# Gate and up of 19 of 22 feature tiles by seven block products of a Strassen form

## The chip, the core and the metric

The kernel runs on one core of one Trainium2 chip. The metric is the device time of one execution in microseconds (us), as the median of several runs; the kernel before has 719.12 us (719.12, 715.12 and 721.13). Engines are called as the profile does: PE is TensorE (matmuls), PEld its loading of the stationary operand, DVE VectorE, ACT ScalarE, POOL GpSimd, SP SyncE, whose queue issues the transfers from and to HBM.

## What is computed

One decoder layer over 512 tokens and a width of 1024, in float32: a token mixer (four heads of differential attention and eight of a sparse attention), an output projection, a residual, and a channel mixer. The change concerns the channel mixer alone, which is

```python
x = x + rms_norm(mix, attn_post_norm[l])
h = rms_norm(x, ffn_pre_norm[l])
f = (jax.nn.silu(h @ w_gate[l]) * (h @ w_up[l])) @ w_down[l]
x = x + rms_norm(f, ffn_post_norm[l])
```

with h of 512 x 1024, w_gate and w_up of 1024 x 2816 and w_down of 2816 x 1024.

## The kernel before

**Precision.** Every operand of a large matmul is split in a high part, rounded to the format fp32r, and a low part, the rest; a product is three matmuls: high by high, high by low and low by high. ACT makes the high part of a weight tile (`split_w`, L103 in `to_r`) and DVE the low part (L111).

**Tiles.** The 2816 features are 22 tiles of 128. For a tile, `ff_gate` (L841 to 860) makes gate and up, each with 8 row blocks of 128 of the width and three products: 2 x 8 x 3 = 48 matmuls (L850) of 512 columns, the tokens, with a weight block of 128 x 128 as the stationary operand. Both results lie in a PSUM bank each. Then Exp on ACT (L854), add, reciprocal and a product on DVE (L855 to 857) make silu, L858 multiplies by up, and L859 (ACT) and L860 (DVE) split the result in `ffh` and `ffl`, which are kept for all 22 tiles. Tiles 0 and 1 are made in two halves of 256 tokens, with weights that were loaded and split early (`ws` and `whi`, `wlo` in the rows).

**Ahead of it** stand four token tiles of 128: `norm_post` adds the mixer's parts, normalizes and adds the residual (L797 to 801), `norm_pre` normalizes again (L808 to 814), transposes by PE into two banks `trh` (L819) and splits the transposed tile into `hth` (ACT, L822) and `htl` (DVE, L823), the moving operands of L850. POOL multiplies by the gains (L798, L808). `row_rsqrt` makes the sum of squares (ACT L776, DVE L779) and its root.

**Behind it** `down` (L889) takes the 22 tiles one after the other: 4 token tiles x 2 halves of the width x 3 products, 24 matmuls of 512 columns a tile, in eight banks `acc`. The last three tiles are done row by row, and each finished row of token tiles is normalized and written out.

**Order.** A scheduler orders each engine's instructions by a priority, which is the order of the program save where a block is given a higher one (L801 ff. with `tc.high_priority`); every engine then works through its own list in order, and an instruction that waits holds up those behind it on its engine. Buffers are taken from pools by tag in turn (`raw`, `hi` and `lo` have three each for weights; in PSUM `o` has four banks, `gu` and `tr` two each), and the next user of a buffer waits until the last reader is done. All loads are issued from SP's queue in one order, `wraw` for weights (L96 to 98), 512 KB each.

## Time and profile before

| | |
|---|---|
| median of three runs | 719.12 us (715.12 to 721.13) |
| span of the profiled execution | 717.7 us |
| PE busy | 687.1 us, 96% |
| DVE busy | 487.9 us, 68% |
| ACT busy | 302.3 us, 42% |
| POOL busy | 79.5 us, 11% |
| gate and up of tiles 2 to 21 | 366.35 to 590.35 us |
| down | from 590.35 us |

The profiled execution's own time is its span, 717.7 us, from the first to the last instruction; the runs' times are taken without the profile. "Busy" is the union of the durations of an engine's instructions. A matmul's duration overlaps the next one's, so what one costs is read from the distance of the starts. The granted clock is that part of TensorE's full speed, 2.4 GHz, which the chip allowed in a stretch; 0.50 is 1.2 GHz. In a timeline row, x8 stands for eight instructions that followed one another, the time ahead of the engine is from the first one's start to the last one's end, and square brackets hold the idle time before with what ended it.

### The profile page before, as it was taken

The page shows a single profiled execution, that of the slowest core. Times are in us where ns is not written, and L with a number is a line of the kernel's source. Part 1 is how long each engine was busy: PE and PEld are TensorE (multiplying, and loading weights), DVE is VectorE, ACT ScalarE, POOL GpSimd, SP SyncE. Part 2 cuts the span into 40 slices and gives each one's busy share as a digit, 9 for nine tenths or more (in the row PEclk, how much of TensorE's full clock was granted, in tenths as well). Part 3 has the DMA queues.
Part 4 walks back from the last instruction along what each step waited for, and adds up shares of the span by engine and source line. Part 5 has one row for each costly group of instructions (what it writes and reads, how often), then busy time and mean ns, then how long its engine had stood idle before and what let it go on. Part 6 is the DMA issues. An engine that isn't in the chain of part 4 may idle for free.

```text
span 717.7 us, 9480 instructions
## 1 busy us (share of the span) xinstructions
PE 687.1 (96%) x3553; PEld 568.2 (79%) x3553; DVE 487.9 (68%) x801; ACT 302.3 (42%) x632; POOL 79.5 (11%) x86
## 2 busy tenths in 40 slices
PE   9997999999899988986999999999999999999995
PEld 5976888899688877875988888888888888888884
DVE  4867878886999995769876867768677682222227
ACT  7334444466698965536432232322323322121113
POOL 0000000110854443125100000000000000000000
...
GB/s 315 123 132 287 152 273 309 159 258 45 28 134 60 84 35 5 143 263 1 30 89 88 89 91 106 98 88 89 92 109 94 88 89 89 115 90 88 105 13 117
DMA packets 25981, 83.63 MB, mean 117 GB/s; under 512 B 3408, under 2 KB 4304, under 8 KB 25040
## 3 DMA queue, kind: packets, MB, share of 16 engines
...
## 4 chain that ended last, share of the span: by engine, by line
PE 79%; DVE 12%; ACT 4%; DMA 3%; issue 2%; SPq 0%; DVEq 0%; ACTq 0%
PE gu L850 35%; PE acc L889 15%; PE fm L282 9%; PE dv L356 3%; PE tr L501 2%; PE mixp L676 2%; PE avn L629 2%; PE vg L378 2%; DVE nm L489 2%; PE sc L485 2%; PE sc L486 1%; DMA wraw<-in_wf 1%; PE mix L688 1%; PE av L552 1%; ACT p L491 1%
## 5 line engine op out<-in xcount | busy, mean ns | idle before, releaser
L111 DVE TENSOR_TENSOR wlo<-wraw,whi 128x1024 fp32r<-128x1024 f32 (+2 forms) x96 | 116.4, 1215 | 148.2 <-ACT whi L103 100.8
L103 ACT ACTIVATE whi<-wraw 128x1024 fp32r<-128x1024 f32 (+2 forms) x96 | 100.7, 1052 | 210.5 <-PE gu L850 88.2
L850 PE MATMUL gu<-htl,whi 128*128 128x512 f32 (+1 forms) x352 | 86.3, 385 | 0.0
L850 PE MATMUL gu<-hth,whi 128*128 128x512 f32 (+1 forms) x352 | 86.0, 387 | 0.0
L850 PE MATMUL gu<-hth,wlo 128*128 128x512 f32 (+1 forms) x352 | 85.5, 384 | 0.0
L850 PEld LDWEIGHTS gu<-hth,whi 128*128 128x128 f32 x352 | 64.5, 190 | 14.9 <-ACT hth L822 0.3
L850 PEld LDWEIGHTS gu<-htl,whi 128*128 128x128 f32 x352 | 64.3, 187 | 14.7
L850 PEld LDWEIGHTS gu<-hth,wlo 128*128 128x128 f32 x352 | 64.0, 187 | 14.7
L856 DVE RECIPROCAL silu<-silu 128x512 f32<-128x512 f32 (+1 forms) x24 | 74.0, 3085 | 0.7
L510 POOL TENSOR_TENSOR p<-p,l 128x384 f32<-128x384 f32 (+3 forms) x60 | 49.8, 859 | 144.7 <-DVE l L540 88.3
L491 ACT ACTIVATE p<-sc,nm 128x128 f32<-128x128 f32 (+1 forms) x96 | 50.1, 529 | 20.1 <-DVE nm L489 19.7
L889 PE MATMUL acc<-whi,ffl 128*128 128x512 f32 x144 | 56.0, 389 | 0.0
L889 PE MATMUL acc<-wlo,ffh 128*128 128x512 f32 x144 | 56.0, 389 | 0.0
L889 PE MATMUL acc<-whi,ffh 128*128 128x512 f32 x144 | 55.9, 389 | 0.0
L489 DVE TENSOR_REDUCE nm<-sc 128x1 f32<-128x128 f32 (+1 forms) x96 | 42.5, 482 | 10.4 <-PE sc L487 7.1
L282 PE MATMUL fm<-xh,whi 128*128 128x512 f32 x128 | 34.7, 411 | 5.7 <-ACT whi L103 5.2
L505 ACT ACTIVATE pth<-tr 128x384 fp32r<-128x384 f32 (+1 forms) x60 | 31.5, 526 | 16.8 <-PE tr L501 16.6
L506 DVE TENSOR_TENSOR ptl<-tr,pth 128x384 fp32r<-128x384 f32 (+1 forms) x60 | 34.9, 592 | 3.3 <-ACT pth L505 2.9
L485 PE MATMUL sc<-kst,qst 128*128 128x128 f32 (+2 forms) x96 | 35.3, 368 | 1.5 <-DVE pc L586 1.2
L501 PE MATMUL tr<-ident,p 128*128 128x128 f32 x200 | 33.0, 276 | 1.7 <-DVE ptl L506 0.9
L282 PEld LDWEIGHTS fm<-xh,whi 128*128 128x128 f32 x128 | 24.6, 196 | 12.0 <-ACT whi L103 5.8
L282 PE MATMUL fm<-xh,wlo 128*128 128x512 f32 x128 | 33.4, 393 | 0.0
...
## 6 DMA issues: line engine op xcount, KB each, us to landing
wraw<-in_wg SPq DMA_DIRECT2D x22, 512.0 KB, 3.3
wraw<-in_wu SPq DMA_DIRECT2D x22, 512.0 KB, 3.3
wraw<-in_wd SPq DMA_DIRECT2D x22, 512.0 KB, 3.3
wraw<-in_wf SPq DMA_DIRECT2D x16, 512.0 KB, 5.0
...
wraw<-in_wo SPq DMA_DIRECT2D x8, 512.0 KB, 4.1
```

What stands on the lines that cost most here:

```text
L103: act.activation(dst, src, AF.Copy)
L111: (lo_eng or dve).tensor_tensor(lo[:, :w], raw[:, :w], f32(hi[:, :w]), OP.subtract)
L282: pe.matmul(pt, w[:, k * P:(k + 1) * P], xx[k], start=(n == 0), stop=(n == 3 * NK - 1))
L485: pe.matmul(sv, lhs, kk[:, 0, :w], start=True, stop=False)
L489: dve.tensor_reduce(nm, sv, AX.X, OP.max, negate=True)
L491: act.activation(pt, sv, AF.Exp, bias=nm, accum_out=l[:, i:i + 1])
L501: pe.transpose(tr[:, n * P:(n + 1) * P], pts[i][:, j * P:(j + 1) * P], ident)
L506: dve.tensor_tensor(ptl[:, sl], trv, f32(pth[:, sl]), OP.subtract)
L510: pool.tensor_tensor(p, p, l.to_broadcast(list(p.shape)), OP.mult)
L850: pe.matmul(pt, w_col(ww, k), hx[:, k, s0:s1], start=(n == 0), stop=(n == 3 * NK - 1))
L856: dve.reciprocal(sl, sl)
L889: pe.matmul(acc[i][c], a[f][:, i * P:(i + 1) * P], w[wi][:, c * SEQ:(c + 1) * SEQ], start=(first and n == 0), stop=(last and n == 2))
```

## The change

**Seven products.** For tiles 3 to 21 the width is cut in two halves (c = 0, 1) and the tokens in two halves of 256. The blocks of h are A11, A12 (first tokens; first and second half of the width), A21 and A22; b11 and b21 are gate's weights for the two halves of the width, b12 and b22 up's. Winograd's form of Strassen's product gives the four results from seven products of half the width and half the tokens with

- t1 = b12 - b11, t2 = b22 - t1, t3 = b22 - b12, t4 = b21 - t2 for every tile's weights (`ff_prep`, DVE),
- s1 = A21 + A22, s2 = s1 - A11, s3 = A11 - A21, s4 = A12 - s2 once (`h_sums_a`, `h_sums`, DVE and ACT).

Each product is `block_mul` (L905 to 915): 4 row blocks x 3 parts = 12 matmuls of 256 columns (L912), so 84 for a tile where there were 48 of 512 columns. In the text products 1 to 7 are those of `ff_seven` in its order: b11, t1, b21, t2, t4, b22, t3. They accumulate into the halves of two banks x and y; between them ACT copies three partial results out of x and one out of y (L959, L962, L965, L969), and DVE adds banks and copies (L967, L970). The products' order is fixed by a chain of ordering edges, which are not waits.

**Silu** is now the activation of that name, in `ff_gate` (L897) and, for the product tiles, one tile late (`tail`, L976, behind the next tile's L970). Its table is loaded on ACT before the first one and left after the last one (L980).

**Weights.** ACT and DVE now split t2|t1, t3|b22 and b11|b21 (1024 columns each) and t4 (512): four high parts (L933) and four low parts (L934) for a tile. gate's weights still go through `wraw`; up's go to buffers `wu` that share the tag `ru` with the gains; `t21` shares its two with the `u` of the norms. x2 is written to HBM (`x2d`) and read back for the last sum, so that its four buffers serve as weights in between (tag `big`, eight). The gated results stay unsplit (`ffr`) and are split in the down stage (`down_operands`). Tiles 0 to 2 are made as before.

```diff
+NB = {"big": 8, "ru": 2, "t21": 2}
...
-    def work(name):
-        return A.tile([P, D_MODEL], F32, tag="work", name=name, bufs=4)
     g_post, g_pre = gain(0), gain(1)
-    x2 = [A.tile([P, D_MODEL], F32, name=f"x2_{i}") for i in range(NT)]
+    x2 = [big(f"x2_{i}") for i in range(NT)]
...
+    def h_sums_a(i):
+        a21, a22 = trs[i + 2]
+        hr = [f32(sslot("hr")) for _ in range(2)]
+        for c in range(2):
+            h_, l_ = (f32(t[:, 4 * c:4 * c + 4, i * P:(i + 1) * P]) for t in (hth, htl))
+            dve.tensor_tensor(hr[c].rearrange("p (k t) -> p k t", t=P), h_, l_, OP.add)
+        s1, s3 = (f32(sslot("s")) for _ in range(2))
+        dve.tensor_tensor(s3, hr[0], a21, OP.subtract)
+        act.activation(s1, a21, AF.Copy)
+        dve.tensor_tensor(s1, s1, a22, OP.add)
+        raw4[i] = hr, s1, s3
+    def h_sums(i):
+        hr, s1, s3 = raw4[i]
+        s2, s4 = (f32(sslot("s")) for _ in range(2))
+        dve.tensor_tensor(s2, s1, hr[0], OP.subtract)
+        dve.tensor_tensor(s4, hr[1], s2, OP.subtract)
+        raw4[i] = s3
+        h_split(i, (0, s1), (1, s2), (3, s4))
+    def h_split(i, *js):
+        for j, s in js:
+            h_, l_ = (t[:, :, i * P:(i + 1) * P] for t in sums[j][1])
+            sv = s.rearrange("p (k t) -> p k t", t=P)
+            act.activation(h_, sv, AF.Copy)
+            dve.tensor_tensor(l_, sv, f32(h_), OP.subtract)
+    ffr = [None] * NF
...
-        sl = A.tile([P, SEQ], F32, tag="silu", name="silu", bufs=2)[:, s0:s1]
-        act.activation(sl, pts[0][:, s0:s1], AF.Exp, scale=-1.0)
-        dve.tensor_scalar_add(sl, sl, 1.0)
-        dve.reciprocal(sl, sl)
-        dve.tensor_tensor(sl, sl, pts[0][:, s0:s1], OP.mult)
+        sl = ffr[f][:, s0:s1]
+        with tc.issue_after(getattr(last_exp[0], "ins", last_exp[0])):
+            act.activation(sl, pts[0][:, s0:s1], AF.Silu)
         dve.tensor_tensor(sl, sl, pts[1][:, s0:s1], OP.mult)
-        act.activation(ffh[f][:, s0:s1], sl, AF.Copy)
-        dve.tensor_tensor(ffl[f][:, s0:s1], sl, f32(ffh[f][:, s0:s1]), OP.subtract)
+    def ht_block(t0, c):
+        return [[t[:, 4 * c + k, t0:t0 + HT] for k in range(4)] for t in (hth, htl)]
+    before = [None]
+    def block_mul(pt, w, h, start=False):
+        with ExitStack() as es:
+            if before[0] is not None:
+                es.enter_context(tc.issue_after(before[0]))
+            n = 0
+            for ww, hx in ((w[0], h[0]), (w[0], h[1]), (w[1], h[0])):
+                for k in range(4):
+                    m = pe.matmul(pt, ww[:, k * P:(k + 1) * P], hx[k], start=(start and n == 0),
+                                  stop=(n == 11), skip_group_check=True)
+                    n += 1
+        before[0] = getattr(m, "ins", m)
+    prep = {}
+    def ff_prep(f):
+        rg, ru, t21 = load_w(wg[f]), big("wu", tag="ru"), big("t21", tag="t21")
+        nc.sync.dma_start(ru, wu[f])
+        (b11, b21), (b12, b22) = halves(rg), halves(ru)
+        (t2, t1), t3, t4 = halves(t21), b12, f32(sslot("t4"))
+        ops = prep[f] = {}
+        def operand(names, hl):
+            for j, n in enumerate(names):
+                ops[n] = [t[:, j * SEQ:(j + 1) * SEQ] for t in hl]
+        def split(src, hi, lo):
+            act.activation(hi, src, AF.Copy)
+            dve.tensor_tensor(lo, src, f32(hi), OP.subtract)
+            return hi, lo
+        dve.tensor_tensor(t1, b12, b11, OP.subtract)
+        dve.tensor_tensor(t2, b22, t1, OP.subtract)
+        def home(odd):
+            if f % 2 == odd:
+                return split_slots()
+            return big("wh", F32R), big("wl", F32R)
+        operand(("b11", "b21"), split(rg, *home(1)))
+        dve.tensor_tensor(t3, b22, b12, OP.subtract)
+        dve.tensor_tensor(t4, b21, t2, OP.subtract)
+        operand(("t2", "t1"), split(t21, *home(1)))
+        operand(("t3", "b22"), split(ru, *home(0)))
+        operand(("t4",), split(t4, sslot("t4h"), sslot("t4l")))
+    def ff_seven(f):
+        ops = prep.pop(f)
+        x, y = wide(("o", "gu", "o", "tr")[f % 4], "gw")
+        cy, cx = (f32(sslot(n)) for n in ("cy", "cx"))
+        s1, s2, s3, s4 = (q[0] for q in sums)
+        lo, hi = slice(0, HT), slice(HT, SEQ)
+        block_mul(x[:, lo], ops["b11"], ht_block(0, 0), True)
+        act.activation(cy[:, hi], x[:, lo], AF.Copy)
+        block_mul(y[:, lo], ops["t1"], s1, True)
+        block_mul(y[:, hi], ops["b21"], ht_block(0, 1))
+        act.activation(cx[:, lo], y[:, lo], AF.Copy)
+        block_mul(x[:, lo], ops["t2"], s2)
+        block_mul(x[:, hi], ops["t4"], ht_block(HT, 1))
+        act.activation(cy[:, lo], x[:, lo], AF.Copy)
+        block_mul(y[:, lo], ops["b22"], s4)
+        dve.tensor_tensor(cy, y, cy, OP.add)
+        block_mul(x[:, lo], ops["t3"], s3)
+        act.activation(cx[:, hi], x[:, lo], AF.Copy)
+        dve.tensor_tensor(cx, x, cx, OP.add)
+        if late:
+            late.pop()()
+        def tail():
+            for sl, c in ((lo, cy), (hi, cx)):
+                last = act.activation(c[:, hi], c[:, hi], AF.Silu)
+                dve.tensor_tensor(ffr[f][:, sl], c[:, lo], c[:, hi], OP.mult)
+            if f == NF - 1:
+                with tc.issue_after(getattr(last, "ins", last)):
+                    act.preload_act_table_set("natural_log_exp_and_others")
+        late.append(tail)
...
+    x2d = dram.tile([NT, P, D_MODEL], F32, name="x2d")
+    for i in range(NT):
+        nc.sync.dma_start(x2d[i], x2[i])
...
     ff_gate(0, w0, 0, 256, "gu")
     ff_gate(1, w1, 0, 256, "o")
-    ff_gate(0, w0, 256, SEQ, "gu")
-    ff_gate(1, w1, 256, SEQ, "o")
-    for f in range(2, NF):
-        ff_alloc(f)
-        ff_gate(f, ff_weights(f), 0, SEQ, ("gu", "o", "tr", "o")[f % 4])
+    with tc.issue_after(getattr(scaled[0], "ins", scaled[0])):
+        for i in range(2):
+            h_sums_a(i)
+    ff_gate(0, w0, 256, SEQ, "o")
+    ff_gate(1, w1, 256, SEQ, "gu")
+    for i in range(2):
+        h_sums(i)
+    ffr[2] = f32(sslot("ff2"))
+    w2 = ff_weights(2)
+    ff_prep(3)
+    ff_gate(2, w2, 0, SEQ, "o")
+    for i in range(2):
+        h_split(i, (2, raw4[i]))
+    for f in range(3, NF):
+        ffr[f] = f32(sslot(f"ff{f}"))
+        if f < NF - 1:
+            ff_prep(f + 1)
+        ff_seven(f)
+    late.pop()()
...
+    def down_operands(f):
+        w = split_w(load_w(wd[f]))
+        hi, lo = sslot("ffh"), sslot("ffl")
+        to_r("a", hi, ffr[f])
+        dve.tensor_tensor(lo, ffr[f], f32(hi), OP.subtract)
+        return w, hi, lo
...
+    for i in range(NT):
+        x2[i] = big("x2")
+        nc.sync.dma_start(x2[i], x2d[i])
```

**What stands where, PE.** In the steady state PE had, for one tile, these rows; `hth`, `htl` are h's parts, whi and wlo gate's (bank gu_4497), then up's (gu_4498):

```order
L850 MATMUL gu_4497<-hth_3691,whi_4487 128x512 x8
L850 MATMUL gu_4497<-htl_3692,whi_4487 128x512 x8
L850 MATMUL gu_4497<-hth_3691,wlo_4488 128x512 x8
L850 MATMUL gu_4498<-hth_3691,whi_4493 128x512 x8
L850 MATMUL gu_4498<-htl_3692,whi_4493 128x512 x8
L850 MATMUL gu_4498<-hth_3691,wlo_4494 128x512 x8
```

Now the second half of a tile's row reads as follows: product 4 (t2 by s2, rope_3969), product 5 (t4 by A22), product 6 (b22 by s4, hs_3970) and product 7 (t3 by s3); gw_4713 is bank x, gw_4714 bank y:

```order
L912 MATMUL gw_4713<-rope_3969,wh_4576 128x256 x8
L912 MATMUL gw_4713<-rope_3969,wl_4577 128x256 x4
L912 MATMUL gw_4713<-hth_3695,t4h_4584 128x256 x4
L912 MATMUL gw_4713<-htl_3696,t4h_4584 128x256 x4
L912 MATMUL gw_4713<-hth_3695,t4l_4585 128x256 x4
L912 MATMUL gw_4714<-hs_3970,whi_4580 128x256 x4
L912 MATMUL gw_4714<-hs_3971,whi_4580 128x256 x4
L912 MATMUL gw_4714<-hs_3970,wlo_4581 128x256 x4
L912 MATMUL gw_4713<-hth_3695,whi_4580 128x256 x4
L912 MATMUL gw_4713<-htl_3696,whi_4580 128x256 x4
L912 MATMUL gw_4713<-hth_3695,wlo_4581 128x256 x4
```

Products 4, 5 and 7 go into bank x and 6 into bank y, and product 7 (into the half of x that 4 wrote) is the tile's last.

**ACT.** Before, a tile's list on ACT was Exp, one high part, the split of the tile before, one high part:

```order
L854 ACTIVATE silu_4619<-gu_4569 128x512
L103 ACTIVATE whi_4703<-wraw_4701 128x1024
L859 ACTIVATE ffh7_4555<-silu_4619 128x512
L103 ACTIVATE whi_4709<-wraw_4707 128x1024
L854 ACTIVATE silu_4691<-gu_4641 128x512
```

Now a tile's list has eleven rows; here from the end of one tile (banks gw_4713) to that of the next (gw_4838, gw_4839); `cy` and `cx` are the copies, rows L933 make high parts for the tile two further on, and L976 are the Silus of the tile before:

```order
L933 ACTIVATE whi_4830<-wu_4814 128x1024
L969 ACTIVATE cx_4716<-gw_4713 128x256
L959 ACTIVATE cy_4840<-gw_4838 128x256
L976 ACTIVATE cy_4715<-cy_4715 128x256
L976 ACTIVATE cx_4716<-cx_4716 128x256
L933 ACTIVATE whi_4945<-wraw_4937 128x1024
L962 ACTIVATE cx_4841<-gw_4839 128x256
L933 ACTIVATE whi_4951<-t21_4940 128x1024
L933 ACTIVATE t4h_4959<-t4_4942 128x512
L965 ACTIVATE cy_4840<-gw_4838 128x256
L933 ACTIVATE wh_4955<-wu_4939 128x1024
```

The copy of L965, which reads the half of x that product 4 wrote, stands behind three high parts and cx's copy of L962; it is emitted behind product 5, which writes the same bank, and waits for its end.

**DVE ahead of the tiles.** Before, the last token tile's residual (x2_3) was followed by the reciprocal of tile 0 and then by that token tile's sum of squares (ss_3929):

```order
L801 SCALAR_TENSOR_TENSOR x2_3_3686<-u_3876,rs_3885,x2_3_3686 128x512 x2
L855 TENSOR_SCALAR silu_4013<-silu_4013 128x256
L856 RECIPROCAL silu_4013<-silu_4013 128x256
L779 TENSOR_TENSOR ss_3929<-ss_3929 128x1
L823 TENSOR_TENSOR htl_3692<-trh_3915,hth_3691 128x4x128
L857 TENSOR_TENSOR silu_4013<-silu_4013,gu_3963 128x256
L122 TENSOR_SCALAR rr_3934<-ss_3929 128x1
L823 TENSOR_TENSOR htl_3692<-trh_3916,hth_3691 128x4x128
```

Now three operand sums for tile 3 (L937, L938, L945) stand between them, and behind the scaling of that token tile (mixt_3879) come the sums for s1 to s4, before the low part of its first transposes (trh_3949):

```order
L810 SCALAR_TENSOR_TENSOR x2_3_3690<-u_3880,rs_3889,x2_3_3690 128x512 x2
L937 TENSOR_TENSOR t21_4236<-wu_4235,wraw_4233 128x512
L938 TENSOR_TENSOR t21_4236<-wu_4235,t21_4236 128x512
L945 TENSOR_TENSOR wu_4235<-wu_4235 128x512
L786 TENSOR_TENSOR ss_3933<-ss_3933 128x1
...
L825 SCALAR_TENSOR_TENSOR mixt_3879<-x2_3_3690,rs_3937,gain_3685 128x512 x2
L898 TENSOR_TENSOR ff0_3972<-ff0_3972,gu_3975 128x256
L856 TENSOR_TENSOR hr_4078<-hth_3695,htl_3696 128x512
L856 TENSOR_TENSOR hr_4079<-hth_3695,htl_3696 128x512
L858 TENSOR_TENSOR s_4083<-hr_4078,trh_3919 128x512
L834 TENSOR_TENSOR htl_3696<-trh_3949,hth_3695 128x4x128
```

The sum of squares moved behind work that needs `wu_4235`, a load into the buffer of the first gain, and s_4083 (L858, s3 of the first token tile) reads the bank trh_3919, from the pair of banks that trh_3949 takes next.

## Rows read from the trace of the kernel before

**Rows 1.** The page: its first lines, with busy time, share of the span and instructions of each engine, and the granted clock in 40 slices.

```profile
PE 687.1 (96%) x3553; PEld 568.2 (79%) x3553; DVE 487.9 (68%) x801; ACT 302.3 (42%) x632; POOL 79.5 (11%) x86
```

**Rows 2.** The chain of waits from 300 us on, two of its rows: start, duration, engine, tile, line.

```profile
355.04 235.47 PE gu L850 x1056
590.51 110.20 PE acc L889 x486
```

**Rows 3.** The windows by stage (second halves of tiles 0 and 1; tile 2; tiles 3 to 21; down): length, busy time of each engine (instructions), granted clock, DMA share and GB/s.

```profile
core 0: us, PE busy (x) PEld busy (x) DVE busy (x) ACT busy (x) POOL busy (x), PEclk, DMA share, GB/s
355.04:366.35 11.31, 11.31 (x97) 11.31 (x97) 8.17 (x12) 3.84 (x6) 0.00 (x0) 1.00 0.19 53
366.35:377.55 11.20, 11.20 (x51) 9.00 (x49) 8.82 (x11) 3.56 (x5) 0.00 (x0) 1.00 0.28 90
377.55:590.35 212.80, 212.80 (x914) 170.91 (x912) 152.87 (x134) 63.64 (x76) 0.00 (x0) 1.00 0.29 94
590.35:700.71 110.36, 110.36 (x488) 91.39 (x487) 26.06 (x23) 20.79 (x20) 0.00 (x0) 1.00 0.25 81
```

**Rows 4.** The timeline of PE from 338 us: matmuls of 256 columns (tiles 0 and 1, second tokens) and of 512 columns (tile 2).

```profile
356.08 1.09 PE L850 MATMUL gu<-hth,ws 128*128 128x256 f32 x8
357.02 1.09 PE L850 MATMUL gu<-hth,whi 128*128 128x256 f32 x8
357.95 1.09 PE L850 MATMUL gu<-hth,ws 128*128 128x256 f32 x8
...
366.35 2.03 PE L850 MATMUL gu<-hth,whi 128*128 128x512 f32 x8
368.22 2.03 PE L850 MATMUL gu<-htl,whi 128*128 128x512 f32 x8
370.08 2.03 PE L850 MATMUL gu<-hth,wlo 128*128 128x512 f32 x8
```

**Rows 5.** The groups of instructions by line and form from 355.04 to 590.35 us, those of DVE and ACT that recur in the change: count, busy time, mean ns of one, and the idle time before them.

```profile
L856 DVE RECIPROCAL silu<-silu 128x512 f32<-128x512 f32 x20 | 67.0, 3352 | 0.7
L111 DVE TENSOR_TENSOR wlo<-wraw,whi 128x1024 fp32r<-128x1024 f32 x41 | 50.2, 1224 | 50.0 <-PE gu L850 47.4 <-ACT whi L103 2.6
L103 ACT ACTIVATE whi<-wraw 128x1024 fp32r<-128x1024 f32 x42 | 44.5, 1059 | 88.2 <-PE gu L850 88.2
L858 DVE TENSOR_TENSOR silu<-silu,gu 128x512 f32<-128x512 f32 x19 | 12.9, 680 | 0.0
L860 DVE TENSOR_TENSOR ffl<-silu,ffh 128x512 fp32r<-128x512 f32 x16 | 11.1, 693 | 11.2 <-ACT ffh L859 11.2
L859 ACT ACTIVATE ffh<-silu 128x512 fp32r<-128x512 f32 x16 | 10.1, 633 | 43.1 <-DVE silu L858 43.1
L859 ACT ACTIVATE ffh<-silu 128x256 fp32r<-128x256 f32 x3 | 1.3, 418 | 6.3 <-DVE silu L858 6.3
L857 DVE TENSOR_TENSOR silu<-silu,gu 128x256 f32<-128x256 f32 x3 | 1.2, 410 | 0.0
L854 ACT ACTIVATE silu<-gu 128x256 f32<-128x256 f32 x2 | 0.8, 384 | 1.6 <-PE gu L850 1.6
```

**Rows 6.** The timeline of DVE from 400 us, operations back to back.

```profile
399.59 0.69 DVE L857 TENSOR_TENSOR silu<-silu,gu 128x512 f32<-128x512 f32 x1
400.20 1.22 DVE L111 TENSOR_TENSOR wlo<-wraw,whi 128x1024 fp32r<-128x1024 f32 x1
401.35 0.68 DVE L858 TENSOR_TENSOR silu<-silu,gu 128x512 f32<-128x512 f32 x1
```

**Rows 7.** Transfers: the page's list of DMA issues, and that of 300 to 360 us; the last number is the median us from issue to landing.

```profile
wraw<-in_wu SPq DMA_DIRECT2D x22, 512.0 KB, 3.3
...
gain<-in_grow SPq DMA_DIRECT2D x3, 512.0 KB, 7.2
```

**Rows 8.** The timelines of PE, DVE and POOL from 338 to 358 us, ahead of the steady state.

```profile
339.10 3.79 PE L850 MATMUL gu<-hth,ws 128*128 128x256 f32 x16 [2.98 <-ACT hth L822]
...
353.73 1.29 PE L819 MATMUL trh<-ident,mixt 128*128 128x128 f32 x8
355.04 1.20 PE L850 MATMUL gu<-hth,whi 128*128 128x256 f32 x8
...
347.84 1.75 DVE L856 RECIPROCAL silu<-silu 128x256 f32<-128x256 f32 x1
349.51 0.10 DVE L779 TENSOR_TENSOR ss<-ss 128x1 f32<-128x1 f32 x1
...
352.83 1.41 DVE L814 SCALAR_TENSOR_TENSOR mixt<-x,rs,gain 128x512 f32<-128x512 f32 x2
...
338.64 2.98 POOL L798 TENSOR_TENSOR u<-mixt,gain 128x512 f32<-128x512 f32 x2
341.57 1.28 POOL L808 TENSOR_TENSOR u<-x,gain 128x512 f32<-128x512 f32 x1
```

**Rows 9.** The groups of ACT over the span: the load of an activation table (count, busy us, mean ns).

```profile
L166 ACT ACT_TABLE_LOAD x1 | 1.3, 1283 | 0.7 <-PEq L990 0.7
```

**Rows 10.** The windows of line 850 alone, behind the idle time of rows 8: length, busy time of PE and PEld, granted clock, DMA share and GB/s.

```profile
339.10:342.69 3.59, 3.59 (x17) 3.59 (x17) 0.50 0.02 8
```

**Rows 11.** The timeline of PE from 20 to 32 us: matmuls of 256 columns of another line, first and last of six rows and the next.

```profile
25.92 0.64 PE L356 MATMUL dv<-whi,xh 128*128 128x256 f32 x4
...
28.31 0.64 PE L356 MATMUL dv<-whi,xl 128*128 128x256 f32 x4
28.79 0.64 PE L356 MATMUL dv<-wlo,xh 128*128 128x256 f32 x4
```

More of the change, by code (lines that the diff above doesn't have):

```diff
@@ L105, in to_r, with split_slots @@
             dve.tensor_copy(dst, src)
+    def split_slots():
+        return [wpool.tile([P, 1024], F32R, tag=t, name="w" + t, bufs=b) for t, b in (("hi", WB[1]), ("lo", WB[2]))]
     def split_w(raw, w=1024, lo_eng=None, hi_eng="a"):
-        hi = wpool.tile([P, 1024], F32R, tag="hi", name="whi", bufs=WB[1])
-        lo = wpool.tile([P, 1024], F32R, tag="lo", name="wlo", bufs=WB[2])
+        hi, lo = split_slots()
         to_r(hi_eng, hi[:, :w], raw[:, :w])
@@ L131, in hybrid_block_kernel @@
     S = ctx.enter_context(tc.tile_pool(name="s", bufs=NS, side="left"))
+    pad = ctx.enter_context(tc.tile_pool(name="pad", bufs=1, side="left"))
+    pad.tile([P, 8], F32, name="pad")
     R = ctx.enter_context(tc.tile_pool(name="r", bufs=2, side="left"))
@@ L750, in hybrid_block_kernel, with big @@
     A = ctx.enter_context(tc.tile_pool(name="a", bufs=1, side="right", reuse_waits="tile"))
+    def big(name, dt=F32, tag="big"):
+        return A.tile([P, D_MODEL], dt, tag=tag, name=name, bufs=NB[tag])
     def gain(j):
-        t = A.tile([P, D_MODEL], F32, tag="gain", name="gain", bufs=2)
+        t = big("gain", tag="ru")
         nc.sync.dma_start(t, grow[j].partition_broadcast(P))
@@ L791, in hybrid_block_kernel @@
     mixt, us = [None] * NT, [None] * NT
+    hraw = [None] * NT
     def norm_post(i, mix):
-        mixt[i], us[i] = work("mixt"), work("u")
+        mixt[i], us[i] = big("mixt"), big("u", tag="t21")
         m, u, x_ = halves(mixt[i]), halves(us[i]), halves(x2[i])
@@ L823, in norm_pre, with sum_alloc @@
             dve.tensor_tensor(d_l, tv, f32(d_h), OP.subtract)
-    ffh, ffl, ffw = [None] * NF, [None] * NF, []
-    def ff_alloc(f):
-        for j, (l, n) in enumerate(((ffh, "ffh"), (ffl, "ffl"))):
-            k = 2 * f + j
-            if k < NS:
-                l[f] = sslot(f"{n}{f}")
-            else:
-                k -= NS
-                if k % 4 == 0:
-                    ffw.append(rope_tile())
-                l[f] = ffw[-1][:, k % 4]
+        trs[i] = tr
+    sums, raw4, trs = [], [None, None], [None] * NT
+    def sum_alloc():
+        for j in range(4):
+            if j < 2:
+                t = rope_tile().rearrange("p (s k) t -> p s (k t)", s=2)
+                full = [t[:, s].rearrange("p (k t) -> p k t", t=HT) for s in range(2)]
+            elif j == 2:
+                full = [t[:, :4, HT:] for t in (hth, htl)]
+            else:
+                full = [big("hs", F32R).rearrange("p (k t) -> p k t", t=HT) for _ in range(2)]
+            sums.append(([[t[:, k] for k in range(4)] for t in full], full))
+    def h_sums_a(i):
[23 more added lines that the diff above has]
+    ffr = [None] * NF
     def w_col(w, k):
@@ L862, in hybrid_block_kernel @@
+    late = []
     w0, w1 = st["F0"], st["F1"]
```

29 lines of the change are left out of this document (17 added, 12 removed).

## The prediction

> **What bounds the kernel now.** The page's first rows [rows 1] show TensorE (PE) busy for 687.1 of 717.7 us; the chain of waits says where that decides the end. From 355.04 to 700.7 us its two rows are all PE: 235.47 us of gate and up (L850) and 110.20 us of down (L889) [rows 2]. The windows by stage confirm it: from 355.04 on PE is busy in every microsecond at a granted clock of 1.00, while DVE is busy for 152.87 of 212.80 us and ACT for 63.64 [rows 3]. So a matmul taken out of that stage is time taken out of the kernel, as long as DVE and ACT, which get more to do, stay ahead.
>
> What a matmul costs I read from starts, since durations overlap. Of 512 columns, eight start every 1.866 us (366.35, 368.22, 370.08), 0.2333 us each; of 256 columns, with the same stationary tiles and half the tokens, eight start every 0.933 us (356.08, 357.02, 357.95), 0.1167 us each [rows 4]. Half the columns cost half the time.
>
> **The product tiles.** A tile had 48 matmuls of 512 columns: 48 x 0.2333 = 11.20 us, which is also its step from 366.35 to 377.55 in the windows [rows 3]. It now has 7 products of 12 matmuls of 256 columns: 84 x 0.1167 = 9.80 us, 1.40 us a product. Gain 1.40 us on each of 19 tiles: **-26.6 us**. Tiles 0 to 2 keep their matmuls, and the down stage keeps its 528.
>
> The Trainium skill speaks against this: TensorE: Matmul & The Clock Gate, Back-to-back issue gap, gives a sustained 81 ns at 128 columns and 131 ns at 512, so that narrow matmuls cost more per column. An estimate from these two figures by a straight line, 98 ns at 256 columns, would make the tile 8.2 us against 6.3, a loss of 1.9 us a tile. The trace differs: 0.2333 us at 512 and 0.1167 at 256.
>
> **Does DVE hold the pace?** Per product tile it has: t1 to t4, t4's low part and the two sums over a bank (L967, L970), 7 operations of 512 columns at 0.68 to 0.69 us; three low parts of 1024 at 1.224; two products of 256 at 0.41 [rows 5]: 5 x 0.69 + 2 x 0.68 + 3 x 1.224 + 2 x 0.41 = 9.3 us. Gone are Exp's follow-up with the reciprocal (3.35 us), and two of three 512-column products and splits. Back to back they start closer than they last: the 0.69 us one at 399.59 is followed at 400.20, the 1.22 us one there at 401.35 [rows 6], so 0.61 and 1.15: 7 x 0.61 + 3 x 1.15 + 2 x 0.35 = 8.4 us. Both are under 9.80. The one loop through DVE and ACT: ACT's high part of the gate weights (L933) releases on DVE three low parts, three sums, t4's low part and both bank sums, in that order, 7.1 us; then the second Silu, 0.4; then the next tile's high part, 1.06: 8.6 us, 1.2 under the tile.
>
> **Does ACT hold the pace?** Per tile 3 x 1.059 + 0.633 + 4 x 0.384 + 2 x 0.418 = 6.2 us of 9.80 [rows 5]. Silu is not in the trace; bounds for 256 columns are the nearest rows, 0.384 (Exp from a bank) and 0.418 (Copy from SBUF), and I take the second, which has its operand's place. What matters is ACT's order. Product 7 (t3) accumulates into the half bank that cy's copy (L965) reads, so PE waits for that copy. On ACT there stand ahead of it the gate weights' high part, which waits for the end of product 3 (it overwrites the buffer read there), cx's copy, t21's high part and t4h. From the end of product 3: 1.059 + 0.384 + 1.059 + 0.633 + 0.384 = 3.52 us, against products 4 to 6, 3 x 1.40 = 4.20, less 0.16 by which the last matmul of a run outlasts its slot (1.09 against 0.933 [rows 4]): **0.5 us to spare**. The copy's own wait, for product 5, ends 2 x 1.40 + 0.16 later, and 0.384 behind that is 3.34, less than 3.52. So I price the copies at nothing; their cover is those three products, and what it costs without cover is the third rival. Product 4 overwrites what L959 copied two products earlier, and the bank sums have until the bank comes round, four tiles later.
>
> Transfers: a tile loads two times 512 KB as before, 3.3 us to landing [rows 7]. wu now has two buffers; its load is issued when the low part of the tile two before is read, about 2.3 us into a tile, and is wanted at about 6.5: it lands at 5.6.
>
> **The front.** Here the change costs time. Before, PE was at full supply from 355.04, when the last token tile's transposes (353.73) were through [rows 8]. Now DVE works on t21, t1, t3 of tile 3 ahead of the sum of squares of token tile 3. Their wu uses gain g_post's buffer, free after POOL's last multiply by it; POOL's last operations lie at 338.64 to 342.85 [rows 8], so the load comes at 342.9 + 3.3 = 346.2 and three operations end at 348.3, against 349.51 for that sum before: hidden behind the reciprocal that is gone. mixt of token tile 3 ends at about 352.2 (before 354.24). But its first four transposes now want the bank that s1's copy and s3 (L858) of token tile 0 still read: one product of 256 and three of 512 columns later, 0.4 + 3 x 0.65 = 2.3 us, 354.6, plus ACT's copy, about 354.9 to 355.6 against 353.73. PE resumes 1.2 us later (**+1.2**); the second four transposes come apart, 0.47 us and an idle 0.7 (**+1.2**); the added table load, 1.28 us on ACT [rows 9], stands in that chain, of which I take 0.5 (**+0.5**). Sum **+2.9**. I put the front at 0 at the least (PE has 16 matmuls of the next tiles to put in while it would wait) and at 6.8 at the most (a wu that lands after 7.2 us, as gain's does [rows 7], is 3.9 later, with DVE behind it). PE's granted clock may fall where it idles: after 2.98 idle us it was 0.50 for 3.59 us [rows 8, 10], 1.8 us lost; I expect no idle as long.
>
> **To the down stage.** Its operands' split has moved there. The first, ffh of tile 0, stands on ACT behind the last tile's first Silu, which waits for DVE's sum over the bank of product 6; before, PE went on without a gap at 590.35 [rows 3]. 0.16 + 0.68 + 0.418 + 0.633 = 1.89 us after product 6, of which product 7 covers 1.40: 0.5, with the steps from engine to engine **+0.6** (0 to 2). Per down tile ACT then has 1.059 + 0.633 and DVE 1.224 + 0.693 of 24 x 0.227 = 5.4 us: covered. x2's four reloads stand on SP ahead of the fourth down load and wait there for buffers of product tiles 20 and 21; the first three down tiles, 16 us, cover that, and the rows are wanted 90 us later. The tail is the same.
>
> **Sum.** -26.6 + 2.9 + 0.6 = -23.1 us: 717.7 becomes 694.6 for a profiled execution. The span stood 1.4 under the median of its three runs (715.12 to 721.13), so **696.0** as a median.
>
> **Rivals.**
> A. Narrow matmuls cost more than half. The 256-column ones of L356 start 24 in 2.87 us, from 25.92 to 28.79 [rows 11], 0.1196 each: 84 x 0.1196 = 10.05 us, gain 1.15, so 19 x 0.25 = 4.7 us dearer: 700.8. Against it: these rows run on other operands; the gate's own show 0.1167. (The tile gains nothing from 48 x 0.2333 / 84 = 0.1333 us each.)
> B. DVE becomes the bound. 9.3 us with no overlap and 0.1 us at each of its 12 operations, such as waits for ACT leave, is 10.5 us a tile: 0.7 x 19 = 13.3 more: 709.3. For it: 95% of 9.80 by the means; against it the overlap in rows 6.
> C. The other side: PE waits for the copies out of its own banks. If each of the four in a tile were exposed, matmul's end 0.16 and copy 0.384, that is 0.544 x 4 = 2.18 us a tile, 41 us: 737. It decides from 23.1 / 19 = 1.2 us a tile; product 7 (L968) at L965 is its place, where ACT's chain would have to be 1.7 us longer than 3.52.
> D. The front takes its most, 6.8 us, by a wu load that lands after 7.2 us as gain's did [rows 7]: 696.0 + 3.9 = 699.9.
>
> The Trainium skill, PSUM — Partial Sum Buffer, PSUM bank collisions raise a hardware error, wants readers and writers of a bank kept apart by bank and not by address. By that rule copies of one half would hold up matmuls into the other half of the bank, which is rival C's condition; no row of the kernel before shows such a pair.
>
> **Chances.** Forecast 0.58 (own range 692 to 699: front and down step 0 to 6.5 together), A 0.13, B 0.12, C 0.10 (half of it under 1.2 us a tile), D 0.07. From 690 (no cost in front, a run 2 us under) to 711 (B) holds all but C and a part of B, over 0.8. What this measurement can tell from no change is about 1%, 7.2 us: faster, under 711.9, is forecast, A, D and most of B, 0.86; the rest of B and C's small half within, 0.08; slower 0.06.
>
> **What would show it.** Right: 84 matmuls in 9.8 us from tile to tile at clock 1.00, PE idle nowhere between tile 3 and the last, tile 3 starting at 379.8 to 380.5 (before, 377.55), the last down matmul about 23 us earlier. A: starts 0.1196 apart and no idle. B: idle before L912 ended by L934 or L946 on DVE, DVE above 95% in the stage. C: idle before L912 ended by L965, L959 or L962 on ACT. The forecast is wrong if the tile step is over 10.2 us, or PE's idle in front of tile 3 over 8.

## The result, and the profile after

The changed kernel takes 696.66 us (median of 4 runs, 696.04 to 698.13) against 718.49 us of the kernel before (4 runs beside it): ratio 0.9705, 95% interval 0.9665 to 0.9744. Faster, as forecast, and 0.7 us from the forecast of 696.0. The profiled execution has a span of 695.3 us, 22.4 less than before. The sum came out as forecast, but not all of its terms did: the product tiles gain less than forecast, and the front costs less.

The page's first rows, to be set beside [rows 1]: PE is 25 us less busy, DVE and ACT more.

```profile
PE 662.0 (95%) x4237; PEld 585.9 (84%) x4237; DVE 507.7 (73%) x918; ACT 365.3 (53%) x775; POOL 79.0 (11%) x86
```

The windows by stage (columns as in [rows 3]): the product tiles but for their last 0.7 us, and down but for its last 2.4 us. PE is never idle among the product tiles, at a granted clock of 1.00; DVE has 153.05 of 187.70 us, ACT 104.33.

```profile
378.20:565.90 187.70, 187.70 (x1591) 187.69 (x1590) 153.05 (x213) 104.33 (x183) 0.00 (x0) 1.00 0.35 113
...
567.18:684.40 117.22, 117.22 (x517) 97.06 (x518) 43.79 (x62) 38.16 (x60) 0.00 (x0) 1.00 0.23 74
```

The timeline of PE among the product tiles, from tile 4 and tile 5. Four matmuls with the weights wh or wl start every 0.48 us (386.63, 387.11, 387.59), four with whi or wlo every 0.467 (three times from 396.63 to 398.03): 0.12 and 0.1167 us each.

```profile
386.63 0.64 PE L912 MATMUL gw<-hth,wh 128*128 128x256 f32 x4
387.11 0.64 PE L912 MATMUL gw<-htl,wh 128*128 128x256 f32 x4
387.59 0.64 PE L912 MATMUL gw<-hth,wl 128*128 128x256 f32 x4
...
396.63 0.63 PE L912 MATMUL gw<-hth,whi 128*128 128x256 f32 x4
397.10 0.63 PE L912 MATMUL gw<-htl,whi 128*128 128x256 f32 x4
397.57 0.63 PE L912 MATMUL gw<-hth,wlo 128*128 128x256 f32 x4
398.03 0.63 PE L912 MATMUL gw<-hth,whi 128*128 128x256 f32 x4
```

The timelines of PE and ACT ahead of tile 3, which answer to [rows 8]: the last token tile's transposes wait 0.99 us for ACT's copy of s1, and PE then waits twice 0.69 us for ACT's split; tile 3 starts at 378.20 (before: 377.55). The table load at 347.58 delays nothing on this path: ACT sits idle again before the copy of s1, until DVE's L858.

```profile
352.96 0.66 PE L830 MATMUL trh<-ident,mixt 128*128 128x128 f32 x4 [0.99 <-ACT s L859]
354.31 1.20 PE L892 MATMUL gu<-hth,whi 128*128 128x256 f32 x8 [0.69 <-ACT hth L833]
...
358.49 0.74 PE L892 MATMUL gu<-hth,whi 128*128 128x256 f32 x4 [0.69 <-ACT hth L833]
...
378.20 0.63 PE L912 MATMUL gw<-hth,whi 128*128 128x256 f32 x4
```

```profile
347.58 1.28 ACT L897 ACT_TABLE_LOAD   x1
...
352.31 0.60 ACT L859 ACTIVATE s<-trh 128x512 f32<-128x512 f32 x1 [1.32 <-DVE s L858]
```

And the step to down, where PE waits for the first split of the gated results:

```profile
566.15 0.64 PE L912 MATMUL gw<-hth,wl 128*128 128x256 f32 x4
567.18 1.89 PE L1039 MATMUL acc<-whi,ffh 128*128 128x512 f32 x7 [0.39 <-ACT ffh L104]
```

To compare the stages of two executions one needs a mark that the change does not touch. I take the last matmul of avn, in the mixer:

```profile
313.08 0.27 PE L629 MATMUL avn<-ptl,vn 128*128 128x128 f32 x1
```

```profile
311.72 0.27 PE L636 MATMUL avn<-ptl,vn 128*128 128x128 f32 x1
```

The first is of the kernel before, the second of the changed one, 1.36 us earlier. Over all the executions profiled here it lies between 309.75 and 313.82, whichever the kernel, so I put this down to the execution and not to the change. The ledger of the 22.4 us is then:

| stage | before | after | difference | forecast |
|---|---|---|---|---|
| up to the last avn | 313.08 | 311.72 | -1.36 | 0 |
| from there to tile 3 | 64.47 | 66.48 | +2.0 | +2.9 |
| tiles 3 to 21 (378.20 to 566.15 + 0.48) | 212.80 | 188.43 | -24.4 | -26.6 |
| to the first matmul of down | 0 | 0.55 | +0.55 | +0.6 |
| down and end | 127.35 | 128.12 | +0.8 | 0 |

A second execution of the changed kernel (e12 below) repeats all of this but the front: 188.43, 0.54 and 128.1 us, and 66.95 for 66.48. So the front is known to about half a microsecond, +2.0 to +2.5.

### The profile page after: what moved, and what is told of

Same layout as the page of the kernel before. It is cut to its first block, busy times and chain, and to the rows that moved or that the text cites. A ratio compares the mean times of both kernels' runs of the same rounds, so it can differ in the third digit from the quotient of the medians.

```text
span 695.3 us, 11168 instructions
## 1 busy us (share of the span) xinstructions
PE 662.0 (95%) x4237; PEld 585.9 (84%) x4237; DVE 507.7 (73%) x918; ACT 365.3 (53%) x775; POOL 79.0 (11%) x86
## 4 chain that ended last, share of the span: by engine, by line
PE 77%; DVE 12%; ACT 4%; DMA 3%; issue 2%; SPq 0%; DVEq 0%; ACTq 0%
PE gw L912 27%; PE acc L1039 17%; PE fm L289 8%; PE gu L892 4%; PE dv L363 3%; PE mixp L683 2%; PE tr L508 2%; DMA wraw<-in_wf 2%; PE avn L636 2%; PE vg L385 2%; PE sc L492 2%; DVE nm L496 2%; PE mix L695 2%; PE sc L493 1%; PE av L559 1%
## 5 line engine op out<-in xcount | busy, mean ns | idle before, releaser
L114 DVE TENSOR_TENSOR wlo<-wraw,whi 128x1024 fp32r<-128x1024 f32 (+2 forms) x58 | 69.9, 1208 | 83.7 <-ACT whi L104 81.1
L104 ACT ACTIVATE whi<-wraw 128x1024 fp32r<-128x1024 f32 (+2 forms) x58 | 60.5, 1046 | 108.5 <-PE acc L1039 66.6
L1039 PE MATMUL acc<-whi,ffl 128*128 128x512 f32 x176 | 68.5, 389 | 0.0
L1039 PEld LDWEIGHTS acc<-whi,ffh 128*128 128x128 f32 x176 | 33.0, 188 | 7.4 <-ACT ffh L104 0.6
L1039 PEld LDWEIGHTS acc<-wlo,ffh 128*128 128x128 f32 x176 | 33.0, 188 | 6.9
L1039 PEld LDWEIGHTS acc<-whi,ffl 128*128 128x128 f32 x176 | 33.0, 188 | 6.8
L513 DVE TENSOR_TENSOR ptl<-tr,pth 128x384 fp32r<-128x384 f32 (+1 forms) x60 | 34.9, 592 | 2.7 <-ACT pth L512 2.5
L492 PE MATMUL sc<-kst,qst 128*128 128x128 f32 (+2 forms) x96 | 35.4, 369 | 1.5 <-DVE pc L593 1.2
L289 PE MATMUL fm<-xl,whi 128*128 128x512 f32 x128 | 32.8, 392 | 0.0
L493 PE MATMUL sc<-kst,qst 128*128 128x128 f32 (+2 forms) x96 | 31.0, 323 | 0.0
L289 PEld LDWEIGHTS fm<-xl,whi 128*128 128x128 f32 x128 | 23.9, 188 | 5.0
L289 PEld LDWEIGHTS fm<-xh,wlo 128*128 128x128 f32 x128 | 23.7, 188 | 4.7
```

The source lines that it names most:

```text
L104: act.activation(dst, src, AF.Copy)
L114: (lo_eng or dve).tensor_tensor(lo[:, :w], raw[:, :w], f32(hi[:, :w]), OP.subtract)
L289: pe.matmul(pt, w[:, k * P:(k + 1) * P], xx[k], start=(n == 0), stop=(n == 3 * NK - 1))
L492: pe.matmul(sv, lhs, kk[:, 0, :w], start=True, stop=False)
L493: pe.matmul(sv, lhs, kk[:, 1, :w], start=False, stop=False)
L513: dve.tensor_tensor(ptl[:, sl], trv, f32(pth[:, sl]), OP.subtract)
```

## The experiments

One execution of each variant was profiled, and the spans, waits and steps below come from it. Where an interval stands, the variant was also timed several times beside the kernel before, and the ratio is that of the medians; where only a span stands, it rests on that one execution.

**Where the operands lie.** The changed kernel's wh and wl come from the pool of hth and htl, 32 bytes off the place of whi and wlo. e1 moves hth and htl by 32 bytes in the kernel before, with the same instructions:

```diff
+    A.tile([P, 8], F32, name="padA")
     junk = {t: A.tile([P, SEQ], BF16, name="junk" + t, bufs=1) for t in "ab"}
```

> The kernel before, with 32 bytes of padding behind htl in the pool that holds hth and htl, so that both lie at a multiple of 64 bytes in each partition, as the weights' high and low parts do (before: 32 over). Theory 'place': a matmul of 512 columns starts every 0.2267 us where moving and stationary operand have the same remainder by 64 bytes (the down stage) and every 0.2333 where they differ (gate and up); so the 960 gate and up matmuls of tiles 2 to 21 become 0.2267 and the span falls by 960 x 0.0066 = 6.4 us; the 256-column ones of tiles 0 and 1 go from 0.1167 to 0.12 (+0.6 us). Rival 'stage': the spacing belongs to the stage (other engines' traffic), then nothing moves and the time stays within 1 us.

712.32 us, ratio 0.9927 (0.9895 to 0.996). The 20 tiles take 217.60 us (367.60 to 585.20) for 224.0: each of the 960 matmuls of 512 columns starts 0.2267 us after the one before, where it was 0.2333.

```profile
369.44 1.98 PE L852 MATMUL gu<-htl,whi 128*128 128x512 f32 x8
371.25 1.98 PE L852 MATMUL gu<-hth,wlo 128*128 128x512 f32 x8
```

The other engines do the same work in that stage, so the rival 'stage' falls: a shift of 32 bytes alone is worth 6.4 us there. Matmuls of 256 columns go the other way, to 0.96 us for eight (11.61 us for the second halves of tiles 0 and 1, before 11.31 [rows 3]).

**Narrow matmuls.** e2 runs each accumulation of L850 in two halves of 256 tokens:

```diff
+            for h0 in range(s0, s1, 256):
+                pt = pts[wi][:, h0:h0 + 256]
```

> The kernel before, with gate and up of tiles 2 to 21 in matmuls of 256 columns, 96 a tile in place of 48. Theory of the prediction: 96 x 0.1167 = 11.20 us a tile, no change of the span. Rival A: 0.12 each, 11.52 us a tile, +6.4 us. A load of weights that limits narrow matmuls would give more than that; by the estimate from the Trainium skill's two figures (98 ns against 131) the stage would grow by half, over 100 us.

The span is 717.7 us. Eight start every 0.942 us, 0.1178 each; the 20 tiles take 226.1 us (364.24 to 590.38), 11.31 a tile: 0.11 over the theory, under rival A's 11.52, and far from a growth by half. Why it is 0.1178 and not 0.1167 is not known.

```profile
366.12 1.10 PE L851 MATMUL gu<-hth,wlo 128*128 128x256 f32 x8
367.07 1.10 PE L851 MATMUL gu<-hth,whi 128*128 128x256 f32 x8
368.01 1.10 PE L851 MATMUL gu<-htl,whi 128*128 128x256 f32 x8
```

**DVE's room.** e3 puts Exp and the reciprocal back into the product tiles, e8 adds two operations of 512 columns a tile to DVE (`dve.tensor_tensor(junk["b"], t4, rg[:, :SEQ], OP.add)` twice behind the splits of `ff_prep`). The edit of e3:

```diff
-                last = act.activation(c[:, hi], c[:, hi], AF.Silu)
-                dve.tensor_tensor(ffr[f][:, sl], c[:, lo], c[:, hi], OP.mult)
+                last = act.activation(e_, c[:, hi], AF.Exp, scale=-1.0)
+                dve.tensor_scalar_add(e_, e_, 1.0)
+                dve.reciprocal(e_, e_)
+                dve.tensor_tensor(e_, e_, c[:, hi], OP.mult)
+                dve.tensor_tensor(e_, e_, c[:, lo], OP.mult)
```

> The changed kernel, with Exp, add, reciprocal and product in place of the activation Silu in the 19 product tiles. Per tile DVE gets 2 x (0.26 + 1.75 + 0.41) = 4.8 us more, 4.4 back to back, on the 8.06 it is busy: 12.5 us against a step of 9.9. Theory: DVE becomes the bound at 12.2 to 12.9 us a tile, 45 to 57 us more in the span (740 to 752). Rival: DVE's waits add, over 13 us a tile, above 755; or DVE is not needed in time, no change.

> The changed kernel with two operations of 512 columns more on DVE in each product tile (into a junk buffer, same result): 2 x 0.61 to 0.69 on the 8.06 us it is busy of a step of 9.92. Theory: 9.3 to 9.5 us, still under the step, so 0 to 3 us in all, with DVE over 93% busy. Rival B (waits between DVE's operations add about 0.1 us each): over the step at once, 10.5 us a tile, 11 us or more.

e3: span 735.1 us, 39.8 more than the changed kernel, and 736.88 by its own time, a little under the range. DVE is busy in all of the 200 us shown (the first window row). The product tiles take 223.35 us (377.69 to 601.04), 11.76 a tile on average and not 12.2 to 12.9. The steps are uneven, 9.9 to 19.7 us. At their end DVE is behind, and PE waits for the rest of its work in down, until 607.31; with that the 19 tiles come to 12.1 us each, near the range. Of the 34.9 us that the product tiles lose, 24.9 are idle time of PE. The other 10 are matmuls at the lower clock: behind an idle of 6.87 us eight of 256 columns take 1.88 us (475.72 to 477.60) where they took 0.93, at a granted clock of 0.50, and over the stretch the clock is 0.95. So an engine that falls behind costs more here than its waits alone.

```profile
475.72 2.08 PE L912 MATMUL gw<-rope,whi 128*128 128x256 f32 x8 [6.87 <-ACT cy L959]
477.60 1.05 PE L912 MATMUL gw<-rope,wlo 128*128 128x256 f32 x4
...
607.31 0.50 PE L1043 MATMUL acc<-whi,ffl 128*128 128x512 f32 x1 [2.54 <-DVE ffl L1037]
```

e8: span 695.0, tile steps as in the changed kernel, with DVE busy for 92.5% (168.16 of 181.80, the second row):

```profile
400.00:600.00 200.00, 175.59 (x1407) 173.57 (x1407) 200.00 (x286) 90.19 (x164) 0.00 (x0) 0.95 0.28 93
```

```profile
378.20:560.00 181.80, 181.80 (x1542) 181.80 (x1541) 168.16 (x244) 98.65 (x180) 0.00 (x0) 1.00 0.35 114
```

So 9.2 us of work a tile (168.16 of 181.80, for a step of 9.92) do not bind yet, and rival B's extra 0.1 us an operation did not show. And seven products with Exp and the reciprocal would have been slower than the kernel before (735.1 against 717.7 by the spans).

**ACT's room and the copies.** e6 makes t21's high part twice, e7 makes L965's copy six times:

```diff
-        operand(("t2", "t1"), split(t21, *home(1)))
+        operand(("t2", "t1"), split(t21, *home(1), 1))
...
+        for _ in range(6):
+            act.activation(cy[:, lo], x[:, lo], AF.Copy)
```

> The changed kernel with t21's high part made twice, so that ACT has 1.06 us more ahead of L965's copy in each product tile (same result). By the prediction's account (0.5 us to spare on ACT ahead of product 7) PE waits 0.5 us a tile, 10 us in all. By the trace of the changed kernel the copy itself waits 0.44 us a tile for product 5 and ends 0.85 before product 7: 1.3 us to spare, so 0 to 2 us in all.

> The changed kernel with L965's copy made six times in a row: five times 0.32 to 0.385 us, 1.6 to 1.9 us more between product 5's end and product 7 (same result). Rival C's mechanism made to act: product 7 waits for the last of them. Theory: 0.85 us are covered by product 6, so 0.75 to 1.05 us of idle before product 7, ended by L965, in each of 19 tiles: 14 to 20 us more. If PE waits for nothing on ACT there, no change; if a copy of one half also holds up product 6 in the other bank, the whole 1.6 to 1.9 a tile, 30 to 36 us.

e6: span 694.7, nothing lost, so ACT has more to spare than the 0.5 us of the prediction. The trace of the changed kernel says the same: the copy of L965 itself waits for product 5, 8.4 us in 19 tiles, so what stands ahead of it on ACT is done by then (columns: busy, mean ns, idle before).

```profile
L965 ACT ACTIVATE cy<-gw 128x256 f32<-128x256 f32 x19 | 7.3, 385 | 8.4 <-PE gw L912 8.4
```

e7: span 722.2 us, 27 more; the 19 tiles take 214.99 us (379.14 to 594.13) for 188.43. Product 6 (386.14, bank y) is not held up while ACT reads x; product 7 (388.86) waits for the last copy:

```profile
386.14 1.11 PE L912 MATMUL gw<-hs,wh 128*128 128x256 f32 x8
387.09 0.64 PE L912 MATMUL gw<-hs,wl 128*128 128x256 f32 x4
388.86 0.74 PE L912 MATMUL gw<-hth,wh 128*128 128x256 f32 x4 [1.13 <-ACT cy L966]
389.44 0.64 PE L912 MATMUL gw<-htl,wh 128*128 128x256 f32 x4
```

```profile
386.34 2.47 ACT L966 ACTIVATE cy<-gw 128x256 f32<-128x256 f32 x6 [0.42 <-PE gw L912]
```

Six copies take 2.47 us, 0.41 each and not 0.32 to 0.385. PE would have gone on at 387.57 and starts 1.29 us late, and the first four matmuls behind the idle take 0.58 in place of 0.48: 1.4 us a tile, 26.6 in all. That misses the forecast of 14 to 20 and lies under the other one's 30 to 36; the mechanism is the first one's, with a dearer copy. So rival C has its place where the prediction put it, and in the changed kernel about 1.3 us of room keeps it from showing.

**The front.** e4 puts Silu alone into the kernel before, e5 takes the sums s1 to s4 out of the changed one, e10 gives the last token tile's transposes other banks:

```diff
-        act.activation(sl, pts[0][:, s0:s1], AF.Exp, scale=-1.0)
-        dve.tensor_scalar_add(sl, sl, 1.0)
-        dve.reciprocal(sl, sl)
-        dve.tensor_tensor(sl, sl, pts[0][:, s0:s1], OP.mult)
...
+            last_silu[0] = act.activation(sl, pts[0][:, s0:s1], AF.Silu)
...
```

> The kernel before, with the activation Silu alone (table loaded before the first and left after the last) in place of Exp, add, reciprocal and product. Theory: in the tiles PE is the bound and DVE has room, so nothing there; ahead of the tiles the reciprocal of 1.75 us stood before the last token tile's sum of squares, so -1 to -1.5 us, less up to 0.5 for the table load. Rival: Silu carries a good part of the gain, over 5 us.

717.72 us, ratio 0.9992 (0.9969 to 1.0016): no difference that can be told from nothing. In the trace down's matmuls start 276.19 us after avn (309.75 to 585.94), and 277.27 in the kernel before (313.08 to 590.35). The chain of gate and up is 235.47 us long in both [rows 2], so nothing is won in the tiles; the 1.1 us lie ahead of them and have the theory's size, but two executions of one kernel differ there by 0.5.

```diff
-        s1, s2, s3, s4 = (q[0] for q in sums)
+        s1, s2, s3, s4 = ht_block(HT, 0), ht_block(0, 0), ht_block(HT, 0), ht_block(0, 1)
...
-            h_sums_a(i)
...
-        h_sums(i)
...
-        h_split(i, (2, raw4[i]))
...
```

> The changed kernel without s1 to s4: the sums over h's blocks and their splits are left out, and blocks of h itself stand in their place in the products (the results are not those of the layer). Theory: the sums are what the front pays for. Without them the last token tile's eight transposes follow one another and PE loses the waits of 0.99 (for ACT's copy of s1) and 0.69 and the second 0.69 us; from the last matmul of avn to tile 3's first one takes 66.5 us in the changed kernel, 64.5 before; here 63.5 to 64.5. Rival: the wait for wu and the three sums of tile 3 ahead of the last sum of squares, or the table load, are the cost; then it stays at 66 or more. The steps of tiles 4 on are as in the changed kernel, 9.80 to 10.05.

A miss: 68.4 us from avn (311.00) to tile 3 (379.43). The number would suit the rival (66 or more), but the cost is not the one it named. The wait for s1's copy is gone, but with the sums gone DVE's list is ordered otherwise: low parts of weights of 1.2 us each and sums of tiles 3 and 4 stand ahead of the last token tile's scaling, for which PE sits idle 3.30 us.

```profile
348.68 1.21 DVE L934 TENSOR_TENSOR wl<-wraw,wh 128x1024 fp32r<-128x1024 f32 x1
...
353.54 1.40 DVE L825 SCALAR_TENSOR_TENSOR mixt<-x,rs,gain 128x512 f32<-128x512 f32 x2
```

```profile
354.43 1.75 PE L830 MATMUL trh<-ident,mixt 128*128 128x128 f32 x8 [3.30 <-DVE mixt L825]
```

So leaving work out is no clean test where a scheduler fills the gap. e10 keeps the work, gives the transposes banks that the sums do not read, and places them later in the program:

```diff
-TRH = ("tr", "gu", "tr", "tr")
+TRH = ("tr", "gu", "tr", "o")
...
-    with tc.high_priority(offset=HP3):
-        norm_pre(NT - 1)
...
+    ff_gate(1, w1, 0, 256, "o", hold)
+    with tc.high_priority(offset=HP3):
+        norm_pre(NT - 1)
+    for finish in hold:
+        finish()
```

(`hold` keeps the two Silus and their products back until the root has been taken, so that no table is loaded in between.)

> The changed kernel with the last token tile's transposes in two of the banks 'o' in place of 'tr', and emitted behind the first halves of tiles 0 and 1. Theory: in the changed kernel these transposes wait for s1's copy and s3 out of the bank (0.99 us of idle), and are so torn apart that PE idles for ACT's splits twice (0.69 each). Without it one idle of about 0.25 is left: from the last matmul of avn to tile 3's first 64.4 us in place of 66.5, 2.1 us less in the span. Rival: DVE is late there anyway (the low parts of the last transposes, the sums), then PE waits for it at the next place and less than 1 us is won.

> The changed kernel itself, unaltered, beside the three: 696.7 us as before, ratio 0.970; tile 3 starting 66.5 us after the last matmul of avn.

694.35 us, ratio 0.967 (0.9649 to 0.969); the changed kernel beside it on the same chip 697.87, ratio 0.9711 (0.9685 to 0.9737). From avn (310.87) to tile 3 (375.37) it takes 64.5 us; in that second execution of the changed kernel 66.95 (312.59 to 379.54). The transposes follow one another and one idle of 0.25 us is left, as expected. The edit changes banks and order together, so it does not tell one from the other; that the bank is what held the transposes is read from the changed kernel's trace, where the wait ends with L859, a reader of that bank.

```profile
351.57 1.03 PE L830 MATMUL trh<-ident,mixt 128*128 128x128 f32 x8
352.86 0.74 PE L892 MATMUL gu<-hth,whi 128*128 128x256 f32 x4 [0.25 <-ACT hth L833]
```

**Place once more.** e9 moves the shared buffers (wh, wl and hs among them) by 32 bytes, and frees 64 bytes elsewhere, which moves whi and wlo:

```diff
     x2 = [big(f"x2_{i}") for i in range(NT)]
+    A.tile([P, 8], F32, name="padA")
...
-        v, y, t = (cpool.tile([P, n], F32, tag=f"rr{j}{tag}", name="rr", bufs=2) for j in range(3))
+        v, y, t = (cpool.tile([P, n], F32, tag=f"rr{j}{tag}", name="rr", bufs=1 if tag == "c" and j != 1 else 2) for j in range(3))
```

> The changed kernel with the eight shared buffers moved by 32 bytes, so that the weights' parts in them (wh, wl) lie at a multiple of 64 bytes, as whi, wlo and t4h do, while hth, htl and the rope buffers stay 32 over. Theory 'place': products with wh and wl fall from 0.12 to 0.1167 us a matmul; those of product 6, whose moving operand hs moves along, rise to 0.12. In a pair of tiles 72 matmuls are at 0.12 now and 24 then: 48 x 0.0033 = 0.16 us a pair, 1.5 us in 19 tiles. Rival: wh and wl are slow for another reason (their pool, the traffic when they are used): the spacings stay.

697.68 us, ratio 0.9718 (0.9698 to 0.9738): no gain, and the theory of 64 bytes falls. wh and wl went to 0.1175 us, but whi and wlo, which the freed 64 bytes moved from one multiple of 64 to the next, went from 0.1167 to 0.12 with hth and htl; with the rope buffers as the moving operand they stayed at 0.1167 (twelve from 380.57 to 381.97). The 19 tiles take 189.2 us (379.13 to 568.30).

```profile
380.57 1.10 PE L913 MATMUL gw<-rope,whi 128*128 128x256 f32 x8
381.50 0.63 PE L913 MATMUL gw<-rope,wlo 128*128 128x256 f32 x4
381.97 0.64 PE L913 MATMUL gw<-hth,whi 128*128 128x256 f32 x4
...
388.62 0.63 PE L913 MATMUL gw<-hth,wl 128*128 128x256 f32 x4
389.09 0.63 PE L913 MATMUL gw<-hth,wh 128*128 128x256 f32 x4
389.56 0.63 PE L913 MATMUL gw<-htl,wh 128*128 128x256 f32 x4
...
397.58 0.64 PE L913 MATMUL gw<-hth,whi 128*128 128x256 f32 x4
398.06 0.64 PE L913 MATMUL gw<-htl,whi 128*128 128x256 f32 x4
```

> Both edits, the moved buffers and the other banks. Theory: the two add, 1.5 + 2.1 = 3.6 us less than the changed kernel, 693 us where that has 696.7.

e11 has e10's front (64.45 us, 311.85 to 376.30) and e9's tiles: 695.9 us, ratio 0.9677 (0.9652 to 0.9703), no better than e10 alone and not the 693 expected. Of all kernels run here e10's median is the lowest.

## Why the prediction was right, step by step

- **The product tiles** carry the gain: 84 matmuls for 48, with PE alone as the bound. The term was off by 2.2 us of 26.6: it took 0.1167 us for all, where 36 of 84 on average (wh and wl serve 48 in one tile and 24 in the next) have 0.12: 48 x 0.1167 + 36 x 0.12 = 9.92, the measured 188.43 / 19. Rival A came close with 0.1196 for every matmul, from the rows of L356 [rows 11], but for another reason: here it is not the narrow matmul (e2) but where its operands lie (e1, and e9 for wh and wl). Why the rows of L356 have 0.1196 was not tested.
- **DVE** was priced right: 8.4 us back to back forecast, 153.05 of 187.70 us measured, 8.1 a tile. **ACT** has about 1.3 us to spare and not 0.5, a slip that cost nothing: the chain was counted from the end of product 3, but the buffer of the gate weights' high part is free when that product's high by low part is through, one third of a product (0.47 us) ahead of its end, and some of ACT's operations start up to 0.1 us before the one ahead of them ends.
- **The front** was forecast at +2.9 and is +2.0, and +2.5 in the second execution. The first transposes came 0.6 us late (1.1 in the second execution: 354.30, with the last avn at 312.59), not 1.2: mixt ended 38.4 us after avn, 41.2 before. What was misread is [rows 8]: the count let the load of wu wait for POOL's last row, which ended at 342.85. That row (L808) uses the other gain. The last one by the first gain (L798) ended at 341.62, and SP issued the next load into its buffer at 341.65. In the changed kernel POOL was through with it at 339.64, the load went out at 339.67, and the sum of squares behind the three operand sums started at 345.04, not at 348.3. The torn transposes with their two waits of 0.69 cost 1.4 for the 1.2 priced, and the 0.5 for the table load did not occur. Nor did rival D's slow load: wu's loads land after 3.4 us (median of 19). By e10 these costs go when the transposes have other banks and another place.

```profile
341.65 0.33 SPq L754 DMA_DIRECT2D gain<-in_grow  x1
```

```profile
338.36 1.28 POOL L807 TENSOR_TENSOR u<-mixt,gain 128x512 f32<-128x512 f32 x1
339.67 0.33 SPq L923 DMA_DIRECT2D wu<-in_wu  x1
345.04 0.15 DVE L786 TENSOR_TENSOR ss<-ss 128x1 f32<-128x1 f32 x1
348.74 1.41 DVE L825 SCALAR_TENSOR_TENSOR mixt<-x,rs,gain 128x512 f32<-128x512 f32 x2
```

(The first row is of the kernel before, the other four of the changed one.)

- **A sign that did not hold.** Tile 3 was to start at 379.8 to 380.5. It starts at 378.20, and at 379.56 with the 1.36 us added that are not the change's.
- **The step to down** is 0.55 for 0.6. **Down and end**, forecast at nothing, cost 0.8: 0.1 in its matmuls, 0.6 behind the last of them, of which 0.5 to 0.6 recurs in e10 and e12. Most of it, 0.4 us, lies behind DVE's last operation. From there to the end it is 3.4 to 3.6 us in every kernel with product tiles and 3.0 to 3.1 in the kernel before, e1, e2 and e4, so it belongs to the change; its cause stays open. The rows are of the kernel before (span 717.7) and of the changed one (695.3):

```profile
709.83 0.39 PE L889 MATMUL acc<-wlo,rope 128*128 128x512 f32 x1
713.21 1.42 DVE L907 SCALAR_TENSOR_TENSOR uf<-uf,rs,x 128x512 f32<-128x512 f32 x2
```

```profile
686.79 0.39 PE L1039 MATMUL acc<-wlo,ffh 128*128 128x512 f32 x1
690.37 1.42 DVE L1060 SCALAR_TENSOR_TENSOR uf<-uf,rs,x 128x512 f32<-128x512 f32 x2
```

- That the median fell on 696.7 is partly luck: -24.4 in place of -26.6, and the 0.8 of down, were made up by the front's 0.9 and by 1.36 us at the start that are not the change's.
